# Weight splits of 1024 columns at lowest priority, 1/rms spread by the identity, first block of each FFN in one part

## The chip, the cores and the metric

The kernel runs on one core of a Trainium2 chip. The metric is the device time of one execution in microseconds (us). The engines are TensorE (PE; PEld is its weight load), VectorE (DVE), ScalarE (ACT), GpSimd (POOL) and SyncE (SP, which issues the DMAs).

## The reference

A streaming encoder trunk on 256 tokens of width 1024, in float32. There are two layers; each is FFN, token mixer, FFN, and a gated embedding (PLE). The mixer is latent attention (MLA) in layer 0 and forgetting attention (FoX) in layer 1.

```python
def rms_norm(x, g):
    return x * rsqrt(mean(x * x, -1) + 1e-6) * g

def swiglu(x, w_in, w_out):                  # w_in 1024 x 5632, w_out 2816 x 1024
    gate, up = split(x @ w_in, 2)
    return (silu(gate) * up) @ w_out

h = x
for i in range(2):
    h = h + 0.5 * swiglu(rms_norm(h, ffn_norm[i, 0]), ffn_w_in[i, 0], ffn_w_out[i, 0])
    u = rms_norm(h, mix_norm[i])
    h = h + (mla_mixer(u, ...) if i == 0 else fox_mixer(u, ...))     # 8 heads of 128
    h = h + 0.5 * swiglu(rms_norm(h, ffn_norm[i, 1]), ffn_w_in[i, 1], ffn_w_out[i, 1])
    gate = sigmoid(rms_norm(h, ple_norm[i]) @ ple_w_gate[i])
    h = h + gate * (p[i] @ ple_w_proj[i])
return rms_norm(h, final_norm)
```

## The kernel before

The activations lie transposed: `hT` holds 8 blocks of 128 features (partitions) by 256 tokens. Weights stream from HBM in pieces of at most 128 x 1056, most of them 128 x 1024 (one output block of 128 features, 8 input blocks), in the order of the list `plan`. Each float32 product is made of three: a value is split into `hi` (rounded to float32r) and `lo` (the rest), and hi x hi + lo x hi + hi x lo are added up in PSUM.

`Weights.load` splits a piece in steps of 512 columns: ScalarE writes `whi` (L97), VectorE writes `wlo` = raw - hi (L99). For the pieces of MLA and FoX that stand in `shared`, GpSimd takes the second 512. Up to four pieces are split ahead of the one in use (`AHEAD`), in five pairs of buffers.

The multiplication of a weight block with x (`part`) has two forms. With a PSUM tile of two halves (P, 2, T) each of the 8 k-steps is a 512 column matmul (hi of the weight by hi and lo of x, L228) and a 256 column one (lo of the weight by hi of x, L229); the two halves have still to be added. With a tile (P, T) ("in one part") it is three matmuls of 256 columns (`mm3`, L213 to L215), of which the last is the one that needs lo of x.

`Norm` prepares the normed input while the stage before ends: for each of the 8 blocks, `scaled` writes x times the gain as hi (L270 on ScalarE, or L268 on VectorE where asked) and lo (L271 on VectorE), and `square` (ScalarE, L280) and the sum `acc` (GpSimd, L288) collect the squares. The division by the rms comes behind the matmul. `by_token` sums the squares over partitions with PE (`pst`, L301), makes `v` (L304, VectorE) and `rtok` = 1/rms by token on GpSimd (L306), and, if asked, VectorE writes `dg`, a diagonal matrix for each half of the tokens (L311, twice). `by_column` spreads this over all partitions with one matmul of `ones` by `dg` (`pb`, L315), which ScalarE copies to `rb` (L317).

`ffn` starts with `blocks`: the gate and up block of c = 0 run k-steps 0 to 6 of gate (`pg`), then of up (`pu`), and then the last k-step of both, so that the last block of x may come late. From then on gate and up alternate for c = 1 to 21; `gate_up` multiplies by `rb` (`two`, L328), adds the halves on GpSimd (`gu`, L330), and makes `sg` = silu (L332), `hid` (L334) and its split `hs` (L208, L209). Then 8 output blocks `po` use `hs`. While the first FFN runs, VectorE also computes the rotary tables (`tables`).

In FoX, `project` makes k and q of each head in two halves of the loop (half 0 and half 1): `two` on VectorE (L636), the sum `kqv` on GpSimd (L637); the scores `psc` (L641) need both. At the end of each attention, `ps2` are the output blocks that are added to `hT` (L443).

The order on PE and SP is the order of the program. On VectorE, ScalarE and GpSimd a scheduler sets it, by a simulated timeline and each instruction's priority; each engine then runs its own list in order.

Of the kernel before, what the change touches and what calls it, by code (L numbers as in the profile page):

```python
# [11 lines left out]
F32 = mybir.dt.float32  # L12
# [3 lines left out]
AF = mybir.ActivationFunctionType  # L16
ALU = mybir.AluOpType
AX = mybir.AxisListType

P = 128  # L20
D = 1024
T = 256
KD = D // P
# [38 lines left out]
class Weights:  # L62


    RAW, PAIRS, AHEAD = 6, 5, 4

    def __init__(self, nc, pool, plan, shared):
        self.nc, self.pool, self.plan = nc, pool, plan
        self.shared = shared
        self.got = self.loaded = self.fetched = 0  # L70
        self.live, self.raws, self.pairs = [], {}, {}

# [7 lines left out]
    def load(self, pieces=1, between=None):  # L80
        nc = self.nc
        if pieces > 1:
            raw, src = self.fetch()
        else:
            while self.fetched < min(len(self.plan), self.loaded + self.RAW):
                nc.sync.dma_start(*self.fetch())
            raw = self.raws.pop(self.loaded)
        n = raw.shape[-1]
        hi = self.pool.tile([P, n], F32R, name="whi", bufs=self.PAIRS)
        lo = self.pool.tile([P, n], F32R, name="wlo", bufs=self.PAIRS)  # L90
        for i in range(pieces):
            c = slice(i * n // pieces, (i + 1) * n // pieces)
            if pieces > 1:
                nc.sync.dma_start(raw[:, c], src[:, c])
            for b in range(c.start, c.stop, 512):
                b = slice(b, min(b + 512, c.stop))
                nc.scalar.activation(hi[:, b], raw[:, b], AF.Copy)  # L97
                eng = nc.gpsimd if b.start and self.loaded in self.shared else nc.vector
                eng.tensor_sub(lo[:, b], raw[:, b], hi[:, b].bitcast(F32))  # L99
            if between:  # L100
                between(i)
        self.pairs[self.loaded] = (hi, lo)
        self.loaded += 1

    def ahead(self):
        oldest = min(self.live, default=self.got)
# [20 lines left out]
def trunk(ctx, tc, xT, pT, pos, gains, freq, bf, ffn_in, ffn_out, w_down, w_uq, w_ukv, mla_o,  # L127
# [70 lines left out]
    def tmp(name):  # L198
        return work.tile([P, T], F32, name=name, tag="tmp", bufs=7)

    def bank(name, shape=(P, 2, T)):
        return psum.tile(list(shape), F32, name=name, tag="mm")

    W = Weights(nc, wp, plan, shared)


    def split(hi, lo, src):
        nc.scalar.activation(hi, src, AF.Copy)  # L208
        nc.vector.tensor_sub(lo, src, hi.bitcast(F32))  # L209
# [44 lines left out]
    class Norm:  # L254


        def __init__(self, gain, blocks, dim, tag="u"):
            self.gain, self.dim, self.acc, self.left = gain, dim, None, blocks
            if gain is not None:
                bufs = 2 if tag == "u" else 1  # L260
                self.pair = act.tile([P, 2, blocks, T], F32R, name=tag, bufs=bufs)
# [28 lines left out]

        def block(self, b, src, cuts=(slice(0, T),)):
            if self.gain is not None:
                self.scaled(b, src, cuts=cuts)
            self.square(src, cuts=cuts)

        def by_token(self, columns=True):
            pst = psm.tile([P, 2], F32, name="pst", tag="small")
            accs = [self.acc] if self.gain is not None else [self.acc, self.rest]
            for t in range(2):
                for a in accs:  # L300
                    nc.tensor.matmul(pst[:, t:t + 1], a[:, t * P:(t + 1) * P], ones[:, :1],  # L301
                                     start=a is accs[0], stop=a is accs[-1])
            v = work.tile([P, 2], F32, name="v")
            nc.vector.tensor_scalar(v, pst, 1.0 / self.dim, EPS, op0=ALU.mult, op1=ALU.add)  # L304
            self.rtok = work.tile([P, 2], F32, name="rtok", bufs=3)
            nc.gpsimd.tensor_tensor(self.rtok, v, mhalf, op=ALU.pow)  # L306
            if not columns:
                return
            self.dg = work.tile([P, 2, P], F32, name="dg", bufs=2)
            for t in range(2):  # L310
                nc.vector.tensor_scalar(self.dg[:, t, :], ident, self.rtok[:, t:t + 1], None, op0=ALU.mult)  # L311

        def by_column(self):
            pb = psm.tile([P, T], F32, name="pb", tag="small")
            nc.tensor.matmul(pb, ones, self.dg.rearrange("p a b -> p (a b)"), start=True, stop=True)  # L315
            self.rb = work.tile([P, T], F32, name="rb", bufs=3)
            nc.scalar.activation(self.rb, pb, AF.Copy)  # L317
            self.rb2 = self.rb.rearrange("p (o t) -> p o t", o=1).to_broadcast([P, 2, T])


    def ffn(norm, nxt, meanwhile=None, at=1):
        hs = big.tile([P, 2, KF, T], F32R, name="hs", tag="big")

        def gate_up(c, ps):
            gu = []
            for p in ps:
                two = work.tile([P, 2, T], F32, name="two", tag="pair2", bufs=5)
                nc.vector.tensor_mul(two, p, norm.rb2)  # L328
                gu.append(tmp("gu"))
                nc.gpsimd.tensor_add(gu[-1], two[:, 0, :], two[:, 1, :])  # L330
            sg = tmp("sg")
            nc.scalar.activation(sg, gu[0], AF.Silu)  # L332
            hid = tmp("hid")
            nc.gpsimd.tensor_mul(hid, sg, gu[1])  # L334
            split(hs[:, 0, c, :], hs[:, 1, c, :], hid)

        ps0 = bank("pg"), bank("pu")
        blocks(ps0, norm.pair)
        waits = [(0, ps0)]
        for c in range(1, KF):  # L340
            pg = bank("pg")
            block(pg, norm.pair)
            if c == at:
                norm.by_token()
            pu = bank("pu")
            block(pu, norm.pair)
            if c == at:
                norm.by_column()
            waits.append((c, (pg, pu)))
            if c >= at:  # L350
                for w in waits:
                    gate_up(*w)
                waits = []
            if c == 4 and meanwhile:
                meanwhile()
        for d in range(KD):

            ps = bank("po", (P, 2, T) if d < KD - 1 else (P, T))
            for a in range(0, KF, KD):
                w, = W.get()  # L360
                part(ps, w, hs, range(a, min(a + KD, KF)), KF - 1, at=lambda k: (k - a) * P)
                W.done(w)
            for p in parts(ps):
                nc.vector.scalar_tensor_tensor(hT[:, d, :], p, 0.5, hT[:, d, :], op0=ALU.mult, op1=ALU.add)
            nxt.block(d, hT[:, d, :])
# [110 lines left out]
    def mla(norm, nxt):  # L476
# [48 lines left out]
        for hp in range(H // 2):  # L525
            ps = bank("ps")
            for s in range(2):
                part(ps[:, s, :], w, nkv.pair, range(1), at=lambda k: (2 * hp + s) * P)
            pk.append(ps)
            if hp == 1:  # L530
                nq.by_token(False)

                qscale = work.tile([P, 2], F32, name="qscale", bufs=1)
                nc.vector.tensor_scalar(qscale, nq.rtok, MLA_SCALE, None, op0=ALU.mult)
# [28 lines left out]
    def fox(norm, nxt):  # L563
# [66 lines left out]
        def project(h, half):  # L630
            if (h, half) == (0, 1):
                gates_by_token()
            ps = bank("ps")
            block(ps, norm.pair)
            two = work.tile([P, 2, T], F32, name="two", tag="pair2", bufs=5)
            nc.vector.tensor_mul(two, ps, norm.rb2)  # L636
            nc.gpsimd.tensor_add(kq[:, 2 * h + half, :], two[:, 0, :], two[:, 1, :])  # L637

        def score(h, dst, t):
            n = (t + 1) * P  # L640
# [7 lines left out]
    def ple(i, norm, nxt):  # L648
# [23 lines left out]
        def by_token(d):  # L672
            for t in range(2):
                nc.tensor.transpose(po[t][d // 4][:, d % 4 * P:(d % 4 + 1) * P], hgs[d][:, t * P:(t + 1) * P], ident)
# [26 lines left out]
        if po:  # L701
            by_token(KD - 3)
            by_token(KD - 2)
            nxt.by_token(False)
            by_token(KD - 1)
            for t in range(2):
                for i in range(2):
                    o = work.tile([P, 4 * P], F32, name="o", bufs=5, tag="pair2")
                    r = nxt.rtok[:, t:t + 1]
                    if i == 0:  # L710
                        nc.scalar.activation(o, po[t][i], AF.Copy, scale=r)
                    else:
                        nc.vector.tensor_scalar(o, po[t][i], r, None, op0=ALU.mult)  # L713
                    nc.sync.dma_start(out[t * P:(t + 1) * P, i * 4 * P:(i + 1) * 4 * P], o)
# [201 lines left out]
```

## Time and profile before

| | us |
|---|---|
| median of 3 runs | 1042.16 (1041.62 to 1043.01) |
| profiled execution, its own time | 1040.49 |
| its span | 1038.7 |
| PE / DVE / ACT / POOL busy | 1003.6 / 811.8 / 549.3 / 409.3 |
| granted TensorE clock, mean | 0.991 of full speed |

The profile is of one execution. The rows of busy tenths cut its span into 40 slices of 26 us; each digit is a slice. In the table of waits a row gives the engine, tile and line that waited, what came last, and the us in total, the times, and the longest. In the timeline a row gives start, duration, engine, line, operation and the tiles, output before inputs; xN joins N of a kind, and the brackets give the idle time of the engine ahead of it and what ended it. In the groups the numbers are the total busy time, the mean of one in ns, and the idle time before them.

### The profile page before, as it was taken

What the parts mean: (1) busy time and instruction counts of PE and PEld (TensorE: products, weight loads), DVE (VectorE), ACT (ScalarE), POOL (GpSimd) and SP (SyncE); (2) the same over time, 40 slices, a digit from 0 to 9 for tenths busy, and PEclk for the clock granted to TensorE, in tenths of its full rate; (3) what the DMA queues carried; (4) which work ended last, traced back from release to release, by engine and by line L of the source; (5) the groups of instructions that cost most, each with busy time, mean ns of one, the idle gap of its engine ahead of it and who ended that gap; (6) DMA issues with size and microseconds to landing.
All of it is one profiled execution on the core that took longest, in us unless ns stands there. A gap on an engine that the chain in (4) does not pass through costs nothing. (4 is left out here: it accounts for less than half of the span.)

```text
span 1038.7 us, 17058 instructions
## 1 busy us (share of the span) xinstructions
PE 1003.6 (97%) x6084; PEld 888.0 (85%) x6084; DVE 811.8 (78%) x1367; ACT 549.3 (53%) x1168; POOL 409.3 (39%) x422
## 2 busy tenths in 40 slices
PE   6999999999979999999999999999999799999997
PEld 4888888987868888889888888899888688888896
DVE  8899987576669999766889997765766699997764
ACT  4445555466545554545655555556545455555554
POOL 4629531361326545110255552113664265551102
PEclk9999999999989999999999999999999899999998
DMA  7555666641345665665556656664443456656631
GB/s 274 186 195 159 187 205 199 204 143 61 92 158 180 201 184 185 193 198 166 187 177 202 186 179 181 196 207 149 143 152 113 161 169 198 193 180 194 195 119 42
DMA packets 51973, 179.05 MB, mean 172 GB/s; under 512 B 6064, under 2 KB 6960, under 8 KB 51888
## 3 DMA queue, kind: packets, MB, share of 16 engines
q1 hardware_dynamic: 50880, 176.48, 53.9%
q10 hardware_dynamic: 1008, 1.48, 0.4%
q8 instruction: 48, 0.79, 0.3%
q14 instruction: 37, 0.30, 0.1%
HBM read 176.89 MB, written 1.05 MB: 171 GB/s over the span
## 5 line engine op out<-in xcount | busy, mean ns | idle before, releaser
L99 DVE TENSOR_TENSOR wlo<-raw,whi 128x512 fp32r<-128x512 f32 (+1 forms) x646 | 472.3, 766 | 100.4 <-ACT whi L97 99.3
L97 ACT ACTIVATE whi<-raw 128x512 fp32r<-128x512 f32 (+1 forms) x688 | 382.7, 608 | 235.6 <-issue 81.9
L228 PE MATMUL pg<-u,whi 128*128 128x512 f32 x704 | 255.0, 400 | 20.0 <-DVE u L271 20.0
L228 PE MATMUL pu<-u,whi 128*128 128x512 f32 x704 | 254.3, 399 | 0.0
L330 POOL TENSOR_TENSOR gu<-two 128x256 f32<-128x256 f32 x176 | 169.0, 965 | 182.1 <-DVE two L328 165.8
L228 PE MATMUL po<-hs,whi 128*128 128x512 f32 x616 | 215.2, 393 | 0.9 <-DVE hs L209 0.9
L229 PE MATMUL pg<-u,wlo 128*128 128x256 f32 x704 | 199.9, 284 | 1.5 <-DVE wlo L99 1.5
L229 PE MATMUL pu<-u,wlo 128*128 128x256 f32 x704 | 199.9, 284 | 0.5 <-DVE wlo L99 0.5
L228 PEld LDWEIGHTS pg<-u,whi 128*128 128x128 f32 x704 | 133.4, 189 | 52.9 <-DVE u L271 14.8
L229 PE MATMUL po<-hs,wlo 128*128 128x256 f32 x616 | 173.3, 281 | 0.0
L228 PEld LDWEIGHTS pu<-u,whi 128*128 128x128 f32 x704 | 134.6, 191 | 30.7
L228 PEld LDWEIGHTS po<-hs,whi 128*128 128x128 f32 x616 | 115.7, 188 | 27.4 <-DVE hs L209 1.2
L229 PEld LDWEIGHTS pg<-u,wlo 128*128 128x128 f32 x704 | 133.7, 190 | 3.5 <-DVE wlo L99 3.4
L229 PEld LDWEIGHTS pu<-u,wlo 128*128 128x128 f32 x704 | 134.7, 191 | 1.0 <-DVE wlo L99 1.0
L208 ACT ACTIVATE hs<-hid 128x256 fp32r<-128x256 f32 x88 | 36.8, 418 | 165.3 <-POOL hid L334 165.3
L288 POOL TENSOR_TENSOR acc<-acc,sq 128x256 f32<-128x256 f32 x53 | 46.4, 876 | 187.3 <-ACT sq L280 186.6
L229 PEld LDWEIGHTS po<-hs,wlo 128*128 128x128 f32 x616 | 115.8, 188 | 0.0
L334 POOL TENSOR_TENSOR hid<-sg,gu 128x256 f32<-128x256 f32 x88 | 90.3, 1026 | 24.5 <-ACT sg L332 17.1
L99 POOL TENSOR_TENSOR wlo<-raw,whi 128x512 fp32r<-128x512 f32 x42 | 58.4, 1396 | 64.6 <-ACT whi L97 64.4
L209 DVE TENSOR_TENSOR hs<-hid,hs 128x256 fp32r<-128x256 f32 x88 | 58.7, 667 | 22.9 <-ACT hs L208 20.9
L328 DVE TENSOR_TENSOR two<-pg,rb 128x512 f32<-128x512 f32 x88 | 60.1, 683 | 8.7 <-PE pg L229 8.7
L328 DVE TENSOR_TENSOR two<-pu,rb 128x512 f32<-128x512 f32 x88 | 59.7, 678 | 0.3
(223 smaller groups left out, 1370.9 us busy)
## 6 DMA issues: line engine op xcount, KB each, us to landing
raw<-in_ffn_in_dram SPq DMA_DIRECT2D x174, 512.0 KB, 3.6
raw<-in_ffn_out_dram SPq DMA_DIRECT2D x64, 512.0 KB, 3.5
raw<-in_ffn_out_dram SPq DMA_DIRECT2D x32, 384.0 KB, 3.2
raw<-in_ple_gate_dram SPq DMA_DIRECT2D x16, 512.0 KB, 3.6
raw<-in_fox_qk_dram SPq DMA_DIRECT2D x16, 512.0 KB, 3.5
raw<-in_mla_o_dram SPq DMA_DIRECT2D x8, 512.0 KB, 3.5
raw<-in_fox_o_dram SPq DMA_DIRECT2D x8, 512.0 KB, 3.5
raw<-in_fox_v_dram SPq DMA_DIRECT2D x6, 512.0 KB, 3.4
```

Of the source, the lines that this page charges most:

```text
L97: nc.scalar.activation(hi[:, b], raw[:, b], AF.Copy)
L99: eng.tensor_sub(lo[:, b], raw[:, b], hi[:, b].bitcast(F32))
L208: nc.scalar.activation(hi, src, AF.Copy)
L209: nc.vector.tensor_sub(lo, src, hi.bitcast(F32))
L228: nc.tensor.matmul(ps, hi, x[:, :, k, :], start=k == 0, stop=False)
L229: nc.tensor.matmul(ps[:, 1, :], lo, x[:, 0, k, :], start=False, stop=k == last)
L288: nc.gpsimd.tensor_add(new, self.acc, sq)
L328: nc.vector.tensor_mul(two, p, norm.rb2)
L330: nc.gpsimd.tensor_add(gu[-1], two[:, 0, :], two[:, 1, :])
L334: nc.gpsimd.tensor_mul(hid, sg, gu[1])
```

## The change

Pieces that are loaded whole are split in one step over all their columns, at a priority lowered by 60, except those of `shared` groups and the six behind each (`fine`), which keep 512. `dg` is gone: `by_column` now makes two matmuls of `rtok`, broadcast as the stationary operand, by `ident`. The first gate and up block of each FFN go in one part, so that `gate_up` multiplies them by `rb` straight into `gu`. `Norm.block` has the hi of the last block written by VectorE. In FoX the halves of half 1 are added by VectorE.

```diff
@@ -63,10 +63,13 @@
 
 
     RAW, PAIRS, AHEAD = 6, 5, 4
-
-    def __init__(self, nc, pool, plan, shared):
-        self.nc, self.pool, self.plan = nc, pool, plan
+    LATER = 60
+
+    def __init__(self, tc, pool, plan, shared):
+        self.tc, self.nc, self.pool, self.plan = tc, tc.nc, pool, plan
         self.shared = shared
+
+        self.fine = {i + j for i in shared for j in range(self.AHEAD + 3)}
         self.got = self.loaded = self.fetched = 0
         self.live, self.raws, self.pairs = [], {}, {}
 
@@ -92,15 +95,24 @@
             c = slice(i * n // pieces, (i + 1) * n // pieces)
             if pieces > 1:
                 nc.sync.dma_start(raw[:, c], src[:, c])
-            for b in range(c.start, c.stop, 512):
-                b = slice(b, min(b + 512, c.stop))
-                nc.scalar.activation(hi[:, b], raw[:, b], AF.Copy)
-                eng = nc.gpsimd if b.start and self.loaded in self.shared else nc.vector
-                eng.tensor_sub(lo[:, b], raw[:, b], hi[:, b].bitcast(F32))
+            if pieces > 1:
+                self.split(hi, lo, raw, c, 512)
+            else:
+
+                with self.tc.high_priority(-self.LATER):
+                    self.split(hi, lo, raw, c, 512 if self.loaded in self.fine else n)
             if between:
                 between(i)
         self.pairs[self.loaded] = (hi, lo)
         self.loaded += 1
+
+    def split(self, hi, lo, raw, cut, step):
+        nc = self.nc
+        for b in range(cut.start, cut.stop, step):
+            b = slice(b, min(b + step, cut.stop))
+            nc.scalar.activation(hi[:, b], raw[:, b], AF.Copy)
+            eng = nc.gpsimd if b.start and self.loaded in self.shared else nc.vector
+            eng.tensor_sub(lo[:, b], raw[:, b], hi[:, b].bitcast(F32))
 
     def ahead(self):
         oldest = min(self.live, default=self.got)
@@ -201,7 +213,7 @@
     def bank(name, shape=(P, 2, T)):
         return psum.tile(list(shape), F32, name=name, tag="mm")
 
-    W = Weights(nc, wp, plan, shared)
+    W = Weights(tc, wp, plan, shared)
 
 
     def split(hi, lo, src):
@@ -290,10 +302,10 @@
 
         def block(self, b, src, cuts=(slice(0, T),)):
             if self.gain is not None:
-                self.scaled(b, src, cuts=cuts)
+                self.scaled(b, src, b == KD - 1, cuts=cuts)
             self.square(src, cuts=cuts)
 
-        def by_token(self, columns=True):
+        def by_token(self):
             pst = psm.tile([P, 2], F32, name="pst", tag="small")
             accs = [self.acc] if self.gain is not None else [self.acc, self.rest]
             for t in range(2):
@@ -304,15 +316,12 @@
             nc.vector.tensor_scalar(v, pst, 1.0 / self.dim, EPS, op0=ALU.mult, op1=ALU.add)
             self.rtok = work.tile([P, 2], F32, name="rtok", bufs=3)
             nc.gpsimd.tensor_tensor(self.rtok, v, mhalf, op=ALU.pow)
-            if not columns:
-                return
-            self.dg = work.tile([P, 2, P], F32, name="dg", bufs=2)
-            for t in range(2):
-                nc.vector.tensor_scalar(self.dg[:, t, :], ident, self.rtok[:, t:t + 1], None, op0=ALU.mult)
 
         def by_column(self):
             pb = psm.tile([P, T], F32, name="pb", tag="small")
-            nc.tensor.matmul(pb, ones, self.dg.rearrange("p a b -> p (a b)"), start=True, stop=True)
+            for t in range(2):
+                nc.tensor.matmul(pb[:, t * P:(t + 1) * P], self.rtok[:, t:t + 1].to_broadcast([P, P]), ident,
+                                 start=True, stop=True)
             self.rb = work.tile([P, T], F32, name="rb", bufs=3)
             nc.scalar.activation(self.rb, pb, AF.Copy)
             self.rb2 = self.rb.rearrange("p (o t) -> p o t", o=1).to_broadcast([P, 2, T])
@@ -324,9 +333,12 @@
         def gate_up(c, ps):
             gu = []
             for p in ps:
+                gu.append(tmp("gu"))
+                if len(p.shape) == 2:
+                    nc.vector.tensor_mul(gu[-1], p, norm.rb)
+                    continue
                 two = work.tile([P, 2, T], F32, name="two", tag="pair2", bufs=5)
                 nc.vector.tensor_mul(two, p, norm.rb2)
-                gu.append(tmp("gu"))
                 nc.gpsimd.tensor_add(gu[-1], two[:, 0, :], two[:, 1, :])
             sg = tmp("sg")
             nc.scalar.activation(sg, gu[0], AF.Silu)
@@ -334,7 +346,7 @@
             nc.gpsimd.tensor_mul(hid, sg, gu[1])
             split(hs[:, 0, c, :], hs[:, 1, c, :], hid)
 
-        ps0 = bank("pg"), bank("pu")
+        ps0 = bank("pg", (P, T)), bank("pu", (P, T))
         blocks(ps0, norm.pair)
         waits = [(0, ps0)]
         for c in range(1, KF):
@@ -528,7 +540,7 @@
                 part(ps[:, s, :], w, nkv.pair, range(1), at=lambda k: (2 * hp + s) * P)
             pk.append(ps)
             if hp == 1:
-                nq.by_token(False)
+                nq.by_token()
 
                 qscale = work.tile([P, 2], F32, name="qscale", bufs=1)
                 nc.vector.tensor_scalar(qscale, nq.rtok, MLA_SCALE, None, op0=ALU.mult)
@@ -634,7 +646,7 @@
             block(ps, norm.pair)
             two = work.tile([P, 2, T], F32, name="two", tag="pair2", bufs=5)
             nc.vector.tensor_mul(two, ps, norm.rb2)
-            nc.gpsimd.tensor_add(kq[:, 2 * h + half, :], two[:, 0, :], two[:, 1, :])
+            (nc.vector if half else nc.gpsimd).tensor_add(kq[:, 2 * h + half, :], two[:, 0, :], two[:, 1, :])
 
         def score(h, dst, t):
             n = (t + 1) * P
@@ -701,7 +713,7 @@
         if po:
             by_token(KD - 3)
             by_token(KD - 2)
-            nxt.by_token(False)
+            nxt.by_token()
             by_token(KD - 1)
             for t in range(2):
                 for i in range(2):
```

Three places where the order on VectorE changes. The rows are as the program has them; the line numbers of after are 12 or 13 higher (L99 is L115, L271 is L283, L268 is L280, L304 is L316, L443 is L455, L486 is L498, L636 and L637 are L648 and L649).

VectorE in MLA, where 1/rms is formed, before:

```order
L304 TENSOR_SCALAR v_2399<-pst_2396 128x2 [waits PE_49]
L99 TENSOR_TENSOR wlo_2391<-raw_2201,whi_2390 128x512 [waits DMAHW0_49,Activation_49]
L311 TENSOR_SCALAR dg_2403<-ident_83,rtok_2401 128x128 [waits Pool_49]
L311 TENSOR_SCALAR dg_2403<-ident_83,rtok_2401 128x128
L99 TENSOR_TENSOR wlo_2409<-raw_2230,whi_2408 128x512 [waits DMAHW1_49,Activation_49]
L486 TENSOR_TENSOR cq_2443<-pq0_2328,rb_2431 128x256 [waits Activation_49]
L486 TENSOR_TENSOR cq_2449<-pq1_2329,rb_2431 128x256
```

The same place after:

```order
L316 TENSOR_SCALAR v_2277<-pst_2274 128x2 [waits PE_49]
L115 TENSOR_TENSOR wlo_2269<-raw_2079,whi_2268 128x512 [waits DMAHW0_49,Activation_49]
L115 TENSOR_TENSOR wlo_2284<-raw_2108,whi_2283 128x512 [waits DMAHW1_49,Activation_49]
L498 TENSOR_TENSOR cq_2319<-pq0_2206,rb_2307 128x256 [waits Activation_49]
L498 TENSOR_TENSOR cq_2325<-pq1_2207,rb_2307 128x256
```

The two dg are gone, and the second split stands directly ahead of `cq`.

VectorE at the end of FoX, where the last output blocks become the input of the next FFN, before:

```order
L443 TENSOR_TENSOR hT_78<-ps2_9123,hT_78 128x256 [waits PE_49]
L443 TENSOR_TENSOR hT_78<-ps2_9090,hT_78 128x256 [waits DVE_49]
L99 TENSOR_TENSOR wlo_9162<-raw_8990,whi_9161 128x512 [waits DMAHW4_49,Activation_49,Pool_49]
L99 TENSOR_TENSOR wlo_9162<-raw_8990,whi_9161 128x512 [waits Activation_49]
L271 SCALAR_TENSOR_TENSOR u_7845<-hT_78,g_sb_79,u_7845 128x256 [waits Activation_49] x2
L99 TENSOR_TENSOR wlo_9202<-raw_9016,whi_9201 128x512 [waits DMAHW5_49,PE_49,Activation_49]
```

The same place after:

```order
L455 TENSOR_TENSOR hT_78<-ps2_8713,hT_78 128x256 [waits PE_49]
L455 TENSOR_TENSOR hT_78<-ps2_8680,hT_78 128x256 [waits DVE_49]
L115 TENSOR_TENSOR wlo_8752<-raw_8580,whi_8751 128x512 [waits DMAHW4_49,Activation_49,Pool_49]
L115 TENSOR_TENSOR wlo_8752<-raw_8580,whi_8751 128x512 [waits Activation_49]
L280 TENSOR_SCALAR u_7445<-hT_78,g_sb_79 128x256 [waits DVE_49]
L283 SCALAR_TENSOR_TENSOR u_7445<-hT_78,g_sb_79,u_7445 128x256 [waits Activation_49]
L283 SCALAR_TENSOR_TENSOR u_7445<-hT_78,g_sb_79,u_7445 128x256 [waits DVE_49]
L115 TENSOR_TENSOR wlo_8808<-raw_8606,whi_8807 128x512 [waits DMAHW5_49,Activation_49]
```

The hi of the last block (L280) has come to VectorE, behind the two splits and ahead of the lo of blocks 6 and 7. The place at the end of MLA reads alike.

VectorE in FoX at the first heads, before:

```order
L636 TENSOR_TENSOR two_8227<-ps_8202,rb_7969 128x512 [waits PE_49]
L99 TENSOR_TENSOR wlo_8234<-raw_8067,whi_8233 128x512 [waits DMAHW6_49,Activation_49]
L636 TENSOR_TENSOR two_8255<-ps_8230,rb_7969 128x512 [waits PE_49]
L99 TENSOR_TENSOR wlo_8284<-raw_8101,whi_8283 128x512 [waits DMAHW7_49,Activation_49]
L378 TENSOR_REDUCE m_8265<-psc_8258 128x1 [waits PE_49]
```

The same place after:

```order
L648 TENSOR_TENSOR two_7817<-ps_7792,rb_7561 128x512 [waits PE_49]
L115 TENSOR_TENSOR wlo_7824<-raw_7657,whi_7823 128x512 [waits DMAHW6_49,Activation_49]
L649 TENSOR_TENSOR kqv_7446<-two_7817 128x256 [waits DVE_49]
L648 TENSOR_TENSOR two_7845<-ps_7820,rb_7561 128x512 [waits PE_49]
L115 TENSOR_TENSOR wlo_7874<-raw_7691,whi_7873 128x512 [waits DMAHW7_49,Activation_49]
L390 TENSOR_REDUCE m_7855<-psc_7848 128x1 [waits PE_49]
```

The sum of half 1 (L649) stands behind one split on VectorE; before, it was in GpSimd's list.

## The prediction

> **What bounds the kernel now.** I read the page first, then TensorE's waits, then the timeline around each wait.
>
> ```profile
> PE 1003.6 (97%) x6084; PEld 888.0 (85%) x6084; DVE 811.8 (78%) x1367; ACT 549.3 (53%) x1168; POOL 409.3 (39%) x422
> DVE  8899987576669999766889997765766699997764
> PE pg L228 <- DVE u L271: 20.0, 10, 6.2
> PE pb L315 <- DVE dg L311: 2.2, 1, 2.2
> PE psc L641 <- POOL kqv L637: 2.2, 2, 1.3
> PE pg L229 <- DVE wlo L99: 1.5, 2, 0.8
> PE po L228 <- DVE hs L209: 0.9, 1, 0.9
> ```
>
> TensorE (PE) is busy 97% of the 1038.7 us span. VectorE (DVE) is at 9 tenths or more in the FFN slices, but that costs only where PE waits. The five wait rows (total us, times, longest) come to 26.8 us; 6.2 of them are the start, until the first block of x is split. A weight split (L99) holds PE twice, both at the start, before any weight is ahead. So I sum over PE's waits and PE's own instructions; DVE time saved elsewhere is worth nothing.
>
> **Weight splits of 1024.**
>
> ```profile
> L99 DVE TENSOR_TENSOR wlo<-raw,whi 128x512 fp32r<-128x512 f32 x608 | 456.1, 783 | 100.4 <-ACT whi L97 99.3
> L99 DVE TENSOR_TENSOR wlo<-raw,whi 128x256 fp32r<-128x256 f32 x36 | 18.7, 519 | 0.0
> ```
>
> Mean 783 ns for 512 columns and 519 for 256 is 264 per 256, so a 1024 piece is about 783 + 2 x 264 = 1311, against 1566 for two: 0.255 us less. In the new order 252 splits are 1024 wide, 32 are 768 and 4 cover a 1056 wide pair, so 288 instructions go: at most 73 us of DVE, 7% of the span. No PE wait after the start names wlo, and the four weights kept ahead cover 4 x 8 k-steps of 0.35 us, 11 us. What hides this term is that cover; if it went, each us of lateness would be PE's. Direct worth: 0. Indirectly it helps one place:
>
> ```profile
> 147.12 0.42 DVE L209 TENSOR_TENSOR hs<-hid,hs 128x256 fp32r<-128x256 f32 x1 [1.08 <-ACT hs L208]
> 147.60 0.51 PE L228 MATMUL po<-hs,whi 128*128 128x512 f32 x1 [0.92 <-DVE hs L209]
> ```
>
> This is the first FFN's last hs. DVE has fallen behind there, because the rotary tables share it with 22 hidden blocks (the 9s of the third to fifth slice), and it is still behind here. One hidden block has 2 x 8 x 0.35 = 5.6 us of PE and two weights, four splits before and two now: 0.5 us of DVE less in each of some 20 blocks. 0.92 has to be made up, so I take the wait as gone: -1.0 (-1.2, the wait and the restart behind it, to 0).
>
> **dg removed, 1/rms spread by the identity.**
>
> ```profile
> L311 DVE TENSOR_SCALAR dg<-ident,rtok x18: 275/282/1311, 31.4 to 1004.6; 128x128 f32<-128x128 f32 x18
> 208.46 1.10 POOL L306 TENSOR_TENSOR rtok<-v,mhalf 128x2 f32<-128x2 f32 x1 [2.83 <-DVE v L304]
> 209.53 2.49 POOL L99 TENSOR_TENSOR wlo<-raw,whi 128x512 fp32r<-128x512 f32 x2
> 209.59 2.51 DVE L311 TENSOR_SCALAR dg<-ident,rtok 128x128 f32<-128x128 f32 x2 [0.60 <-POOL rtok L306]
> 209.79 0.28 PE L215 MATMUL pkv<-u,whi 128*128 128x256 f32 x1
> 212.25 0.67 PE L315 MATMUL pb<-dg,ones 128*128 128x256 f32 x2 [2.17 <-DVE dg L311]
> ```
>
> In MLA the two dg rows took 2.51 us beside two POOL splits of 2.49, where 2 x 0.282 is the median. PE's last matmul before pb starts at 209.79 and makes room at 209.91; rtok is ready at 209.56. With rtok as the stationary operand nothing stands between, so 2.17 us go. I take -2.1 (-2.5 with the cold first matmul behind it; -1.5 if rb, cq and q behind it on ACT and DVE show part of the old delay again). Next late is rtok itself, but 0.35 before PE. Elsewhere pb did not wait; the other sixteen dg rows were hidden and give 0.
>
> PE pays for it: one matmul of 256 columns becomes two of 128, each with its own load.
>
> ```profile
> 32.29 0.39 PE L228 MATMUL pu<-u,whi 128*128 128x512 f32 x1
> 32.64 0.59 PE L315 MATMUL pb<-dg,ones 128*128 128x256 f32 x2
> 33.30 0.28 PE L229 MATMUL pg<-u,wlo 128*128 128x256 f32 x1
> 207.68 0.50 PE L301 MATMUL pst<-ones,acc 128*128 128x1 f32 x4
> 208.25 0.28 PE L214 MATMUL pkv<-u,wlo 128*128 128x256 f32 x1
> 208.48 0.28 PE L213 MATMUL pkv<-u,whi 128*128 128x256 f32 x1
> 208.84 0.28 PE L213 MATMUL pkv<-u,whi 128*128 128x256 f32 x1
> 743.93 0.39 PE L641 MATMUL psc<-kqv 128*128 128x128 f32 x2
> 744.15 0.22 PE L642 MATMUL psc<-drop,pick 96*128 96x128 bf16 x1
> ```
>
> From pb's start to the second matmul of the step after it is 0.66; that step's first matmul takes 0.23 of a normal 0.35 (32.29 to 32.64), so pb costs 0.43. Each such matmul of the program leaves two records. Two matmuls with two operands to load stand in pst's four: from 207.68 to the second matmul of the next step at 208.25, less the 0.12 of that step's first (a third of the 0.36 below), is 0.45, with one column each. One of 128 columns is the psc of FOX: 743.93 to 744.15, 0.22; two of them 0.44, and with what pb shows beyond 2 x 0.12 at its end (0.19) 0.63. So pb will cost 0.45 to 0.63, 0.02 to 0.20 more; I take the middle, 0.1. Nine pb (18 dg rows, two each): +0.9 (0 to +1.8).
>
> **First block in one part, last block's hi on VectorE.** Three 256 column matmuls make a k-step of 0.36 (208.48 to 208.84) instead of 0.35: up to 0.01 x 64 steps, +0.3 (0 to +0.6). At the start the third matmul still follows the weights: +0.2 (0 to +0.4). The first two now need only ScalarE's hi; before, the pair waited for lo. The place after FOX, and the same after MLA:
>
> ```profile
> 806.92 0.47 DVE L271 SCALAR_TENSOR_TENSOR u<-hT,g_sb,u 128x256 fp32r<-128x256 f32 x1
> 810.05 1.28 DVE L99 TENSOR_TENSOR wlo<-raw,whi 128x512 fp32r<-128x512 f32 x2
> 811.19 1.59 POOL L288 TENSOR_TENSOR acc<-acc,sq 128x256 f32<-128x256 f32 x2 [2.01 <-ACT sq L280]
> 811.25 1.80 DVE L271 SCALAR_TENSOR_TENSOR u<-hT,g_sb,u 128x256 fp32r<-128x256 f32 x2
> 813.11 0.79 PE L228 MATMUL pg<-u,whi 128*128 128x512 f32 x1 [2.98 <-DVE u L271]
> 813.91 0.63 PE L228 MATMUL pu<-u,whi 128*128 128x512 f32 x1
> 818.28 0.39 PE L228 MATMUL pg<-u,whi 128*128 128x512 f32 x1
> 292.68 0.80 PE L228 MATMUL pg<-u,whi 128*128 128x512 f32 x1 [2.58 <-DVE u L271]
> L268 DVE TENSOR_SCALAR u<-hT,g_sb 128x256 fp32r<-128x256 f32 x4 | 2.9, 734 | 1.4 <-DMA hT<-in_xT_dram 1.4
> ```
>
> Before, PE waits until both lo's end (813.05) and has k-step 6 done at 813.91. Now DVE's order behind the two splits is hi of block 7, lo of block 6, lo of block 7. From 811.33: the hi by the four of its kind at the start 0.73, the lo 0.47 alone or 0.90 beside POOL, so 812.5 to 813.0, and then one small matmul of 0.21 where 0.80 stood: 812.8 to 813.3. Gain 0.6 to 1.1; I take -0.7. If POOL's acc holds the hi as its splits held dg (1.31), lo ends at 813.5 and nothing is won. If both are alone, 812.1 and -1.6. Two places: -1.4 (-3.2 to 0). The Trainium skill, GPSIMD Engine Reference, Key points, says that GpSimd's memory interfaces are shared with VectorE and contend with its two port modes and with instructions of two inputs; the dg rows agree (275 against 1311), and by it the hi beside acc would be held: the case of nothing won.
>
> The PLE to FFN place, where one lo is late:
>
> ```profile
> 510.47 0.51 PE L228 MATMUL pg<-u,whi 128*128 128x512 f32 x1 [1.32 <-DVE u L271]
> ```
>
> DVE's order keeps a 1024 split ahead of that lo and puts the two ge ahead of it too, against two matmuls less behind it: -0.2 (-0.6 to +0.4). gate_up for c = 0 loses two POOL adds, off the path: 0.
>
> **Fox's second half added on VectorE.**
>
> ```profile
> 724.49 0.68 DVE L636 TENSOR_TENSOR two<-ps,rb 128x512 f32<-128x512 f32 x1
> 725.13 1.78 POOL L99 TENSOR_TENSOR wlo<-raw,whi 128x512 fp32r<-128x512 f32 x1
> 726.87 0.73 POOL L637 TENSOR_TENSOR kqv<-two 128x256 f32<-128x256 f32 x1
> 727.65 0.49 PE L641 MATMUL psc<-kqv 128*128 128x128 f32 x2 [0.85 <-POOL kqv L637]
> ```
>
> The two is ready at 725.17, but POOL splits a weight until 726.9. On DVE it follows one split: done about 726.3, before PE arrives at 726.8, so 0.85 goes. The other wait (1.3) begins with a late two on DVE, and POOL was free: there about 0.2 goes. -1.0 (-2.1, both, to +0.3, if DVE's eight adds of about 0.45 delay a row maximum). Queued behind the add are only splits and the next two.
>
> **Sum:** -1.0 -2.1 +0.9 +0.3 +0.2 -1.4 -0.2 -1.0 = -4.3 us. The profiled execution's 1040.49 becomes 1036.2; it stands 1.67 below the median 1042.16, so the prediction is 1037.9. A measurement tells about 0.2%, 2.1 us, from no change.
>
> **Rivals.**
> Clock kept. After the 2.98 wait seven k-steps, 813.91 to 818.28, took 4.37 instead of 7 x 0.35 = 2.45: 1.9 lost, and as much after MLA. If the earlier first matmuls keep the clock up, 1.9 to 3.8 more goes: 1034 to 1036. Against it: the idle stretches before k-steps 4 and 5 remain. The Trainium skill, TensorE: Matmul & The Clock Gate, Part 1, drops the clock after an idle window of about 3.4 us; no single wait here is that long and the clock still fell, so the trace does not agree with a plain reading.
>
> No change. The waits move: POOL's acc holds the hi at both places (0 in place of -1.4), rb stands behind one of ACT's splits in MLA (+0.6, taken as long as one of DVE's at 810.05), pb costs 1.8, fox's second wait grows. Then -1.0 -1.5 +1.8 +0.6 +0.2 +0 -0.5 = about -0.4: 1041.8.
>
> Slower. Lowest priority starves the weights while tables and hidden blocks compete for DVE in the first FFN (9s in slices 3 to 5). It starts to cost when splits come more than the 11 us of cover late, and turns the sign beyond 15.3, the 4.3 gained: at 18 the time is 1037.9 + 7 = 1044.9. For it: DVE has little spare time there. Against: no weight wait occurs in the same stretch now, and DVE's load per block falls by 0.5.
>
> The change does nothing it says: at the attention to FFN places it does not, since the weights there are kept at 512 and the order is the same but for the three last rows; this is in the sum.
>
> **Chances.** My sum 0.60 (own range 1036 to 1040.5), clock kept 0.15, no change 0.17, slower 0.08. Of my sum 0.52 lie more than 2.1 below and 0.08 within; clock kept is all faster; of no change 0.15 is within and 0.02 above: faster 0.67, same 0.23, slower 0.10. The range for 8 in 10 is 1034.2 (clock kept at both places) to 1042.0 (no change).
>
> **What would show it.** pb in MLA starts within 0.3 of the matmul before it; no hs wait near 147; psc waits below 1.3 in sum; the last pg k-step after MLA and FOX ends 1.5 to 2.0 after the last pair of splits instead of 2.6 (813.91 less 811.33); the 1024 split at 1.2 to 1.3 us, with no PE wait on it. Wrong if PE waits for wlo outside the start, or if pb costs over 0.65.

## The result and the profile after

The changed kernel takes 1052.77 us (median of 4 runs, 1052.39 to 1053.58) against 1042.01 (1041.62 to 1043.01). The ratio is 1.0103, with a 95% interval of 1.0085 to 1.012: 10.8 us slower, where 4.3 us faster was forecast.

From the page of the changed kernel, engines and the slices of VectorE and of the granted clock:

```profile
PE 1008.0 (96%) x6166; PEld 896.9 (85%) x6166; DVE 739.4 (70%) x1077; ACT 518.6 (49%) x872; POOL 415.5 (40%) x406
DVE  7798666566567676766877676666886786767654
PEclk9999989999989999999999999999999899999999
```

VectorE lost 72 us of work, some 65 of them in the splits, and of its three slices of 9 in the first FFN one is left. ScalarE lost 31 us. Yet the span grew by 12. A new slice of lower clock stands sixth from the left. TensorE's waits, in the same columns as before:

```profile
PE pg L227 <- DVE u L283: 9.0, 7, 1.5
PE po L240 <- DVE hs L221: 8.5, 4, 4.0
PE pg L226 <- DVE wlo L115: 5.8, 4, 2.4
PE pg L225 <- ACT whi L113: 5.3, 1, 5.3
PE psc L653 <- DVE kqv L649: 3.9, 3, 2.2
PE pg L225 <- ACT u L282: 2.0, 3, 0.8
```

The row of pb is gone, as forecast. The rows of u, wlo and whi together are as long as before (22.1 now, 22.0 before): at the start much the same wait is put down to another cause. All waits together rise from 28.4 to 36.0 us and PE's busy time by 4.4, which is the 12 of the span. The row that carries the loss is the second: po waits for hs at the end of all four FFNs, 8.5 us, where it had waited once, 0.9. And psc waits 3.9 instead of 2.2. At the end of the first FFN the wait also costs the clock:

```profile
152.20 0.79 PE L240 MATMUL po<-hs,whi 128*128 128x512 f32 x1 [3.96 <-DVE hs L221]
153.00 0.63 PE L240 MATMUL po<-hs,whi 128*128 128x512 f32 x1
158.12 0.41 PE L240 MATMUL po<-hs,whi 128*128 128x512 f32 x1
```

From 153.00 to 158.12 eight k-steps took 5.12 us instead of 8 x 0.35 = 2.8: 2.3 more lost, in the slice that the page shows at a lower clock. The granted clock is at half from 151.33 to 158.15.

**Why hs is late.** One hidden block in the second FFN of the changed kernel, timeline rows of VectorE, ScalarE and GpSimd (only those of the path followed here):

```profile
399.31 0.74 POOL L346 TENSOR_TENSOR hid<-sg,gu 128x256 f32<-128x256 f32 x1
400.09 0.42 ACT L220 ACTIVATE hs<-hid 128x256 fp32r<-128x256 f32 x1 [3.19 <-POOL hid L346]
400.41 2.00 ACT L113 ACTIVATE whi<-raw 128x1024 fp32r<-128x1024 f32 x2
401.49 1.23 DVE L115 TENSOR_TENSOR wlo<-raw,whi 128x1024 fp32r<-128x1024 f32 x1 [0.45 <-ACT whi L113]
402.63 0.68 DVE L341 TENSOR_TENSOR two<-pu,rb 128x512 f32<-128x512 f32 x1
403.39 1.65 POOL L342 TENSOR_TENSOR gu<-two 128x256 f32<-128x256 f32 x1 [2.64 <-DVE two L341]
405.12 0.73 POOL L346 TENSOR_TENSOR hid<-sg,gu 128x256 f32<-128x256 f32 x1
```

The rows close a ring. ScalarE has hs ahead of the next weight's whi; VectorE has that weight's wlo ahead of two of up; GpSimd needs that two for gu and then hid, on which the next hs waits. No engine is full, but each runs its list in order, and one turn takes 405.12 - 399.31 = 5.81 us. The same rows of before, where it was catching up in its second FFN:

```profile
335.65 1.08 POOL L334 TENSOR_TENSOR hid<-sg,gu 128x256 f32<-128x256 f32 x1
336.76 0.42 ACT L208 ACTIVATE hs<-hid 128x256 fp32r<-128x256 f32 x1 [2.45 <-POOL hid L334]
337.08 2.18 ACT L97 ACTIVATE whi<-raw 128x512 fp32r<-128x512 f32 x4
337.74 1.28 DVE L99 TENSOR_TENSOR wlo<-raw,whi 128x512 fp32r<-128x512 f32 x2
338.95 0.68 DVE L328 TENSOR_TENSOR two<-pu,rb 128x512 f32<-128x512 f32 x1
339.71 1.12 POOL L330 TENSOR_TENSOR gu<-two 128x256 f32<-128x256 f32 x1 [2.17 <-DVE two L328]
340.90 1.07 POOL L334 TENSOR_TENSOR hid<-sg,gu 128x256 f32<-128x256 f32 x1
```

Here a turn takes 5.25 us. PE needs 5.6 for a block. So before, the ring gained on PE in each block; now it loses 0.2 in each and ends the FFN behind. The turn is steady: start to start of hs in the second FFN, it is 5.80 now (median of 21 turns); before, it was 5.25 until the ring had caught up, and then PE's 5.6. Step by step, start to start: hid to hs 1.11 before, 0.78 now; hs to whi 0.32 in both; whi to wlo 0.66, now 1.08, since VectorE waits for the whole 1024 instead of its first half; wlo to two 1.21, now 1.14; two to gu 0.76 in both; gu to hid 1.19, now 1.73. The last is GpSimd's add, held beside VectorE's split: sorted by whether a split of VectorE overlaps it, the median gu takes 0.74 without one in both kernels (68 and 75 of them), 1.12 beside 512 splits (108, before) and 1.65 beside 1024 splits (89, now). The Trainium skill, GPSIMD Engine Reference, Key points, names this contention with VectorE instructions of two inputs; the rows agree, and they show that the length of the one instruction, not the sum of VectorE's work, is what the add waits out.

### The profile page after: what moved, and what is told of

Same layout as the page of the kernel before. It is cut to its first block, busy times and chain, and to the rows that moved or that the text cites. A ratio compares the mean times of both kernels' runs of the same rounds, so it can differ in the third digit from the quotient of the medians.

```text
span 1050.6 us, 16602 instructions
## 1 busy us (share of the span) xinstructions
PE 1008.0 (96%) x6166; PEld 896.9 (85%) x6166; DVE 739.4 (70%) x1077; ACT 518.6 (49%) x872; POOL 415.5 (40%) x406
## 4 chain that ended last, share of the span: by engine, by line
PE 47%; POOL 20%; issue 19%; DVE 10%; ACT 2%; DMA 0%; POOLq 0%; DVEq 0%; ACTq 0%
POOL gu L342 15%; PE po L240 12%; PE po L241 6%; POOL hid L346 5%; DVE wlo L115 4%; PE ps L240 3%; PE pu L240 3%; PE pg L240 3%; PE ps L241 2%; PE pg L241 2%; PE pu L241 2%; DVE u L283 1%; PE ps L225 1%; PE ps L227 1%; PE ps L226 1%
## 5 line engine op out<-in xcount | busy, mean ns | idle before, releaser
L115 DVE TENSOR_TENSOR wlo<-raw,whi 128x1024 fp32r<-128x1024 f32 (+2 forms) x358 | 406.8, 1140 | 144.5 <-ACT whi L113 142.4
L113 ACT ACTIVATE whi<-raw 128x1024 fp32r<-128x1024 f32 (+3 forms) x400 | 351.1, 910 | 207.1 <-PE po L240 62.1
L342 POOL TENSOR_TENSOR gu<-two 128x256 f32<-128x256 f32 x168 | 197.9, 1182 | 179.9 <-DVE two L341 168.7
L240 PE MATMUL pg<-u,whi 128*128 128x512 f32 x672 | 238.6, 394 | 0.0
L240 PE MATMUL pu<-u,whi 128*128 128x512 f32 x672 | 238.5, 394 | 0.0
L241 PE MATMUL pu<-u,wlo 128*128 128x256 f32 x672 | 189.1, 281 | 0.0
L241 PE MATMUL pg<-u,wlo 128*128 128x256 f32 x672 | 189.0, 281 | 0.0
L240 PEld LDWEIGHTS pu<-u,whi 128*128 128x128 f32 x672 | 126.2, 188 | 28.4
L221 DVE TENSOR_TENSOR hs<-hid,hs 128x256 fp32r<-128x256 f32 x88 | 48.8, 554 | 89.5 <-ACT hs L220 89.5
L115 POOL TENSOR_TENSOR wlo<-raw,whi 128x512 fp32r<-128x512 f32 x42 | 58.7, 1405 | 82.6 <-ACT whi L113 82.5
L346 POOL TENSOR_TENSOR hid<-sg,gu 128x256 f32<-128x256 f32 x88 | 73.5, 835 | 36.4 <-ACT sg L344 29.9
```

The lines of the kernel that those rows point to most:

```text
L240: nc.tensor.matmul(ps, hi, x[:, :, k, :], start=k == 0, stop=False)
L241: nc.tensor.matmul(ps[:, 1, :], lo, x[:, 0, k, :], start=False, stop=k == last)
```

## The experiments

My theory after the result was this ring, set by the width of a split. The rivals were the lowered priority, and the other edits.

### Width undone, the rest of the change kept

```diff
-                    self.split(hi, lo, raw, c, 512 if self.loaded in self.fine else n)
+                    self.split(hi, lo, raw, c, 512)
```

> The changed kernel with every weight split in steps of 512 again, still at the lowered priority; all else of the change kept. Ring theory: in the FFNs hid -> ACT hs -> ACT whi -> DVE wlo -> DVE two(pu) -> POOL gu -> hid closes a ring through three engines that run in order; a 1024 split makes it 5.80 us a block against 5.58 of PE, a 512 split 5.25. So the waits of po for hs (8.5 us, and 2.8 of cold clock behind the longest) go, and the time is 1041 to 1043. Rival, the lowered priority or the rest of the change: the order on VectorE stays, so the waits stay and the time is 1051 to 1053.

1043.89 us against 1042.07, ratio 1.0019 (1.0010 to 1.0029). One hs wait is left (1.8, first FFN); those of FFNs 2 to 4 are gone. The width costs 9 of the 10.8; the rest of the change still costs about 2 (the three edits below sum to -2.5 + 1.4 + 3.7 = 2.6).

### 1024 at low priority alone

Edit: the class `Weights` of the changed kernel (and the argument `tc` that it takes) in the kernel before, nothing else.

> The kernel before with the weight splits of 1024 columns at lowered priority alone. Ring theory: the whole loss stands in it, hs period 5.8 us, hs waits at the end of all four FFNs (about 4, 1.4, 1.7, 1.5 us), time 1051.5 to 1055. Rival, the other parts of the change cost it (VectorE hi, one part, pb): 1041 to 1043.

1062.93 us, ratio 1.0203 (1.0188 to 1.0218): the loss stands in the width, as the ring has it, but it is twice as large as I expected. The hs row of its waits:

```profile
PE po L240 <- DVE hs L221: 12.3, 4, 4.4
```

And the timeline behind the wait of the second FFN:

```profile
434.16 0.80 PE L240 MATMUL po<-hs,whi 128*128 128x512 f32 x1 [2.58 <-DVE hs L221]
437.48 0.39 PE L240 MATMUL po<-hs,whi 128*128 128x512 f32 x1
```

The waits are 2.6 instead of 1.4 to 1.7 in FFNs 2 to 4, and behind each the clock falls now: five k-steps from 434.16 to 437.48 take 3.32 instead of 1.75. The clock also stays at half for 3.4 us behind the wait for dg in MLA (218.95 to 222.36), and at the end of FoX for 10.2 instead of 6.8. In this profile PE is busy for 29.8 us at half clock, in that of before for 9.2 (start and end of the program left out); half of the difference, 10.3, is lost. With the 11.4 more of hs waits that is nearly all of the 22.9 by which the span grew.

### 1024 at normal priority

```diff
-                with self.tc.high_priority(-self.LATER):
-                    self.split(hi, lo, raw, c, 512 if self.loaded in self.fine else n)
+                self.split(hi, lo, raw, c, 512 if self.loaded in self.fine else n)
```

> The changed kernel with the splits at normal priority, 1024 wide as in the change. Ring theory: width alone sets the ring, the same hs period of 5.8 us, time 1050.5 to 1054. Rival, the low priority puts the splits at a bad place: 1042 to 1046.

1051.19 us, ratio 1.0089 (1.0072 to 1.0106), with the same hs waits (8.5, 4, 4.0). Between this and the change the intervals overlap, so priority is not told apart from nothing; width is.

### The ring shortened: up's add on VectorE

```diff
-                nc.gpsimd.tensor_add(gu[-1], two[:, 0, :], two[:, 1, :])
+                (nc.vector if p is ps[1] else nc.gpsimd).tensor_add(gu[-1], two[:, 0, :], two[:, 1, :])
```

> The changed kernel, but the two halves of up are added on VectorE (about 0.45 us) instead of GpSimd (1.66 us beside a 1024 split). Ring theory: the ring falls from 5.80 to about 4.6 us, below PE's 5.58, so hs waits vanish though VectorE has 84 instructions more: time 1039 to 1044. Rival, VectorE's load is what delays hs: waits for hs grow by what the adds take (up to 0.45 a block, some 8 us an FFN), time 1055 or more.

1043.03 us, ratio 1.0006 (0.9996 to 1.0016). There is no hs wait at all, with 84 instructions more on VectorE and 1024 splits kept. The adds, by engine (min, median, max in ns):

```profile
L342 POOL TENSOR_TENSOR gu<-two x84: 728/1607/2443, 38.6 to 938.7; 128x256 f32<-128x256 f32 x84
L342 DVE TENSOR_TENSOR gu<-two x84: 403/424/967, 41.7 to 940.7; 128x256 f32<-128x256 f32 x84
```

GpSimd's adds (of gate) are still held at 1.6 us, but in the ring up's add now takes 0.42 in place of 1.65. This tells the ring from VectorE's load. The turn fell less than I expected, to 5.45 instead of 4.6 (start to start of hs in the second FFN, until PE sets the pace): hid is now itself held beside a split, 1.6 instead of 0.74. So the ring is not opened; its turn is 0.13 below PE's 5.58.

### The other edits, each alone on the kernel before

1/rms spread by the identity:

```diff
-            for t in range(2):
-                nc.vector.tensor_scalar(self.dg[:, t, :], ident, self.rtok[:, t:t + 1], None, op0=ALU.mult)
...
-            nc.tensor.matmul(pb, ones, self.dg.rearrange("p a b -> p (a b)"), start=True, stop=True)
+            for t in range(2):
+                nc.tensor.matmul(pb[:, t * P:(t + 1) * P], self.rtok[:, t:t + 1].to_broadcast([P, P]), ident,
+                                 start=True, stop=True)
```

> The kernel before with 1/rms spread by the identity alone (no dg, two matmuls pb). The wait of 2.2 us for dg in MLA goes with 0.3 of restart, nine pb cost about 0.1 more each: -2.5 + 0.9 = -1.6, so 1039.8 to 1041.2. Rival, the delay shows again as a wait for cq and q: 1042 to 1043.

1039.17 us, ratio 0.9972 (0.9960 to 0.9985): 2.5 us faster by the medians, 1.6 by the spans of the two profiles. What is late next in MLA is a lo of q, 0.4 us:

```profile
PE ps L215 <- DVE q L271: 0.4, 1, 0.4
```

First block in one part and the last block's hi on VectorE:

```diff
-                self.scaled(b, src, cuts=cuts)
+                self.scaled(b, src, b == KD - 1, cuts=cuts)
...
-        ps0 = bank("pg"), bank("pu")
+        ps0 = bank("pg", (P, T)), bank("pu", (P, T))
```

(Left out: in `gate_up`, a tile in one part is multiplied by `rb` straight into `gu`, as in the change.)

> The kernel before with the first FFN block in one part and the last block's hi on VectorE alone. If the start's loss in the changed kernel (its excess over the rhythm 11.6 us against 9.2) is of this edit: start +2.3, the places after MLA and FOX 0 and -1.3 to +1, PLE +0.4: 1043.5 to 1046. Blind prediction's rival: start +0.2, both places -0.7: 1040 to 1042.

1043.01 us, ratio 1.0013 (1.0004 to 1.0022): 1.4 slower, below what I expected. The place after FOX, timeline rows of this kernel:

```profile
812.17 1.28 DVE L99 TENSOR_TENSOR wlo<-raw,whi 128x512 fp32r<-128x512 f32 x2
813.23 1.60 POOL L288 TENSOR_TENSOR acc<-acc,sq 128x256 f32<-128x256 f32 x2 [1.94 <-ACT sq L280]
813.37 0.81 DVE L268 TENSOR_SCALAR u<-hT,g_sb 128x256 fp32r<-128x256 f32 x1
815.17 0.58 PE L215 MATMUL pg<-u,whi 128*128 128x256 f32 x1 [1.53 <-DVE u L271]
815.55 0.41 PE L213 MATMUL pu<-u,whi 128*128 128x256 f32 x1
820.03 0.41 PE L213 MATMUL pg<-u,whi 128*128 128x256 f32 x1
820.67 0.41 PE L213 MATMUL pu<-u,whi 128*128 128x256 f32 x1
```

The hi takes 0.81 ahead of the lo, beside GpSimd's acc; where GpSimd is idle, the same instruction takes 0.35 (at 205.19 in this kernel). This k-step of pg is done, and pu begins, 2.10 after the pair of splits ends (815.55 less 813.45); before, it was 2.58 (813.91 less 811.33). After MLA it is 2.11 against 2.59. So the edit gains 0.5 up to here, just under the forecast 0.6 to 1.1. It does not last: in this execution the clock is at half from 810.72 to 820.96, 10.2 us, where it was 6.8 before (811.30 to 818.12). The k-step from 820.03 to 820.67 still takes 0.64, where before they were back at 0.35 from 818.28 on, and pg and pu are both done 7.7 after the pair in both kernels. In its waits the hs wait of the first FFN has grown from 0.9 to 1.8; why was not tried:

```profile
PE po L228 <- DVE hs L209: 1.8, 1, 1.8
```

FoX's half 1 added on VectorE:

```diff
-            nc.gpsimd.tensor_add(kq[:, 2 * h + half, :], two[:, 0, :], two[:, 1, :])
+            (nc.vector if half else nc.gpsimd).tensor_add(kq[:, 2 * h + half, :], two[:, 0, :], two[:, 1, :])
```

> The kernel before with FoX's half 1 added on VectorE alone. If the order on VectorE (the add stands behind a split, the next head's row maxima behind the add) is what holds psc in the changed kernel (3.9 us against 2.2): +1.5 to +2, 1043.3 to 1044.5. Blind prediction: both waits shrink, -1.0, 1040.5 to 1041.8.

1045.37 us, ratio 1.0021 (1.0010 to 1.0033). Its 11 runs fall into two groups, 4 at 1042.2 to 1042.5 and 7 at 1044.6 to 1045.8; the profiled one is of the second. In it the clock is at half behind the second psc wait (738.13 to 741.55), and at the end of FoX for 10.2 us instead of 6.8. The runs of the first group list a mean clock of 0.990, those of the second 0.987 or 0.988; that they lack one or both of these stretches is likely but not shown. The place in the changed kernel, timeline rows:

```profile
743.11 0.69 DVE L648 TENSOR_TENSOR two<-ps,rb 128x512 f32<-128x512 f32 x1
743.58 1.26 POOL L115 TENSOR_TENSOR wlo<-raw,whi 128x512 fp32r<-128x512 f32 x1 [3.67 <-ACT whi L113]
743.71 1.68 DVE L115 TENSOR_TENSOR wlo<-raw,whi 128x512 fp32r<-128x512 f32 x1
745.31 0.41 DVE L649 TENSOR_TENSOR kqv<-two 128x256 f32<-128x256 f32 x1
745.87 0.46 PE L653 MATMUL psc<-kqv 128*128 128x128 f32 x2 [2.16 <-DVE kqv L649]
```

The add itself is short, but the split ahead of it took 1.68 instead of 0.68, held by GpSimd's split that had begun 0.13 earlier. On GpSimd, before, the add had gone ahead of that split. The other two waits of this row are alike: at 791.87 (1.17) the split ahead took 1.76 beside one of GpSimd, and at 736.54 (0.55) the add itself took 1.51 beside two.

### Two that combine edits

The spread, and up's add on VectorE, at 512 (kernel before otherwise):

> The kernel before with 1/rms spread by the identity, and the halves of up added on VectorE; splits stay at 512. Ring theory: the ring falls below 5.25 us a block, so the one hs wait of before (0.92, first FFN) goes too: -1.6 - 1.2, 1038.5 to 1040.5, faster than both kernels. Rival, VectorE's 88 adds (some 40 us) put it behind in the first FFN beside the tables: hs waits grow, 1042 to 1046.

1039.90 us, ratio 0.9977 (0.9966 to 0.9987). The hs wait is gone from the list, and a wait of 0.8 for a two in the first FFN has come: not told apart from the spread alone.

The spread, and the last block's hi on VectorE, first block in two parts:

> The kernel before with 1/rms spread by the identity and the last block's hi on VectorE, first block in two parts. The lo of block 6 comes ahead of that of block 7, but behind the hi (0.8 us beside GpSimd's acc), so nothing moves at the two places: same as the spread alone, 1038.5 to 1040. Blind prediction: 0.5 less at each place, 1038.0.

1039.05 us, ratio 0.9972 (0.9961 to 0.9983), as the spread alone. With two parts pu begins 2.52 after the pair of splits at both places, 0.06 sooner than before. So the hi on VectorE is worth nothing by itself, and the 1.4 of the edit before are likely of the one part.

### What softens the ring in the whole change

The single edits sum to 21 - 2.5 + 1.4 + 3.7 = +23.6 by the medians (against the kernel before of the same runs); the change costs 10.8. The changed kernel with the first block in two parts:

```diff
-        ps0 = bank("pg", (P, T)), bank("pu", (P, T))
+        ps0 = bank("pg"), bank("pu")
```

> The changed kernel with the first block of each FFN in two parts again. The single edits add up to 22 us and the change costs 10.7, so one edit must soften another. If it is the first block in one part (two GpSimd adds less in the first blocks, so the ring starts less behind): hs waits rise to about 2.6 in FFN 2 to 4 as with 1024 alone, each with 1.5 us of cold clock behind it; time 1058 to 1062. Rival, the FoX add or dg softens it: 1050 to 1053.

1062.18 us, ratio 1.0196 (1.0180 to 1.0211).

```profile
PE po L240 <- DVE hs L221: 12.5, 4, 4.4
```

The one part takes two GpSimd adds out of the ring's first turn. With it the last hs of FFNs 2 to 4 is ready 8.8 to 9.1 us after the first po begins, without it 10.1. So the waits there stay below 1.7 instead of 2.7 and the clock stays up behind them: 9.4 us from an edit that by itself loses 1.4.

And 1024 alone with the ring shortened (the kernel before, `Weights` of the change, up's add on VectorE):

> The kernel before with 1024 splits at lowered priority, and the halves of up added on VectorE. Ring theory: of the 21 us that 1024 costs alone the hs waits (12.3) and the cold clock behind them go; 1041 to 1044. Rival, 1024 costs something besides the ring through GpSimd: 1048 or more.

1042.62 us, ratio 1.0007 (0.9998 to 1.0017).

```profile
PE po L240 <- DVE hs L221: 0.2, 1, 0.2
```

All of the 21 us go with the one add, and then 1024 splits neither gain nor lose, though the splits take some 100 us less of VectorE and ScalarE. One turn in the second FFN of this kernel (some rows between left out):

```profile
340.82 1.59 POOL L346 TENSOR_TENSOR hid<-sg,gu 128x256 f32<-128x256 f32 x1 [0.61 <-DVE gu L342]
342.44 0.42 ACT L220 ACTIVATE hs<-hid 128x256 fp32r<-128x256 f32 x1 [1.78 <-POOL hid L346]
342.89 0.43 DVE L221 TENSOR_TENSOR hs<-hid,hs 128x256 fp32r<-128x256 f32 x1 [1.08 <-ACT hs L220]
343.84 1.23 DVE L115 TENSOR_TENSOR wlo<-raw,whi 128x1024 fp32r<-128x1024 f32 x1
345.70 0.42 DVE L342 TENSOR_TENSOR gu<-two 128x256 f32<-128x256 f32 x1
346.27 1.59 POOL L346 TENSOR_TENSOR hid<-sg,gu 128x256 f32<-128x256 f32 x1 [0.60 <-DVE gu L342]
```

The ring now closes through VectorE's list and hid, and turns in 346.27 - 340.82 = 5.45. It keeps this pace through most of the FFN, so it only just gains on PE.

## Why the prediction was wrong, point by point

- **Splits, "direct worth 0" and hs -1.0.** This step failed. I took the weight's cover of 11 us as all that hides a split, and VectorE's 0.5 us less in each block as a gain for hs. Both look at load and at the weight's own reader. No PE wait on a weight came after the start, as said; but the split also stands ahead of two of up on VectorE and stretches gu on GpSimd, and so lies on the path to hs whatever the load. Measured: hs waits +7.6 us and 2.3 of clock in the change, 21 us for the edit alone. The prediction's own rows held what was needed: 0.28 against 1.31 for dg beside GpSimd's splits. I used that contention at one place and not in the FFN, where 89 of GpSimd's 168 adds run beside a 1024 split.
- **Spread.** Right. The 2.17 wait is gone and the edit alone gives 2.5 (1.6 by the profiles) against the forecast 1.2 (-2.1 + 0.9). The term of nine pb was too large: in the changed kernel

```profile
34.19 0.61 PE L323 MATMUL pb<-ident,rtok 128*128 128x128 f32 x4
34.87 0.28 PE L241 MATMUL pg<-u,wlo 128*128 128x256 f32 x1
```

  so a pb costs 0.68 - 0.23 = 0.45, against 0.43: 0.02 more, the lower bound, 0.2 for nine.
- **First block and hi on VectorE, -1.4 +0.3 +0.2.** Wrong in sign: +1.4. The hi was held by acc, 0.81 instead of 0.35, but no longer than I had priced it, since the four at the start (0.73) had been held too; and pg's last k-step at the two places came 0.5 sooner, where I had taken 0.7. What failed is that I counted this as gained: in the profile the clock came back later behind it, and nothing was left. And I had put two costs too low. The growth of the first FFN's hs wait (+0.9) I had at nothing. For the start I had +0.2: the first po begins at 139.2 to 141.0 in the eight profiles with two parts (mean 139.95) and at 140.25 to 141.2 in the five with one (mean 140.8), so about 0.9 by the means, with a scatter as large.
- **PLE, -0.2.** 0.3 less in the edit alone (1.32 to 1.04); in the change two waits of 1.46 together, 0.1 more.
- **Fox add, -1.0.** Wrong in sign: psc waits 3.9 instead of 2.2. I let a split of 0.68 stand ahead of the add, and did not ask whether GpSimd would be splitting at that moment, for which it was now free.
- **Rivals.** The slower one (0.08) had the right stage, the first FFN, and the wrong mechanism: weights were never late. The clock was not kept at the two places: waits of up to 1.5 us and the fall are still there (half clock from 294.69 to 301.51 and from 820.34 to 827.17); and it fell at a new one. Nor had I read its price right: after MLA seven k-steps took 3.56 (293.49 to 297.05), 1.1 lost and not the 1.9 of FoX.

## What to carry to other kernels

When engines run fixed lists in order, look for a ring: follow one round of the loop from an instruction back to itself through the engines, and compare its turn with the time that the bounding engine takes. Here it was 5.25 against 5.6; a longer instruction at any station, though it saves work in sum, can push the turn over the limit, and then the loss grows with each round. Width is a cost to whoever stands behind or beside the instruction: count the waiting neighbours before merging two short ones.

The best kernels here keep the 512 splits and take only the spread: 1039.2 us, 2.5 less than before, 13.6 less than the change.

## What the runs showed of the hardware

A GpSimd add of 128x256 took 0.74 us alone, 1.12 beside a VectorE split of 512 columns and 1.65 beside one of 1024: an add that began under a split ended 0.60 after that split did, in both kernels (medians of 84 and 79 adds). It goes the other way too: a VectorE split of 512 took 1.68 instead of 0.68 when a GpSimd split had begun 0.13 before it, and a hi of 128x256 took 0.81 beside acc instead of 0.35.

The clock fell behind waits for hs of 2.6 us and more and not behind those of 1.4 to 1.8. But the length of one wait does not decide it: the wait of 2.17 for dg was followed by half clock in the kernel with 1024 alone and not in the kernel before, a psc wait of 2.15 in the FoX edit alone and not one of 2.16 in the change, and after MLA it fell behind two waits of 1.30 and 1.46. In the thirteen profiles each stretch of half clock between the start and the end of the program lasted 3.4, 6.8 or 10.2 us, and the end of FoX alone had 6.8 in some profiles and 10.2 in others. The Trainium skill, TensorE: Matmul & The Clock Gate, Part 1, gives about 3.4 us of idleness for the fall; here 2.15 in one piece was enough.
